# Summing adaLN modulations over partitions with wide ones-matmuls, and fetching their rows earlier

## The chip, the cores and the metric

One Trainium2 chip, one core. The metric is the device time of the program in microseconds (us). Engines are named as in the profile: PE is TensorE (PEld its weight loads), DVE is VectorE, ACT is ScalarE, POOL is GpSimd, SP is SyncE, which here issues DMAs only.

## The reference

A decoder layer with 256 tokens of width 2048, in float32. What matters here is its beginning: a modulation computed from the conditioning vector `c`, applied to the normalised input, and a wide projection of the result.

```python
mod = einsum('bd,de->be', silu(c), w_ada) + b_ada        # w_ada: 2048 x 6144
shift, scale, gate = split(mod[:, None, :], 3, axis=-1)
h = layer_norm(x) * (1.0 + scale) + shift
proj = einsum('bsd,de->bse', h, w_in)                    # w_in: 2048 x 9280
q_lat, kv_lat, mla_gate, pool_in, pool_gate, gate_logits = split(proj, IN_OFFSETS, axis=-1)
...
y = einsum('bsd,de->bse', g_mla * y_mla + g_pool * y_pool, w_out)
x = layer_norm(DEEPNORM_ALPHA * x + (1.0 + gate) * y, ln_g, ln_b)
```

## The kernel before

Each float32 product is made of three fp32r matmuls: an operand is split into a high part (an ACT copy, L108) and a low part (a DVE subtraction, L109), and high x high, high x low and low x high are added up in PSUM (L112 to L114, and with the roles changed L119 to L121).

The 2048 features of `h` are 16 blocks of 128, numbered k = 0 to 15. The product with `w_in` is made in four groups of features, `KGROUPS = ((0, 2), (2, 3), (5, 5), (10, 6))` (first block, number of blocks): here group 0 to group 3. In each group all columns of `w_in` are gone through in blocks of 512; partial sums of earlier groups lie in SBUF and come back into PSUM either by an ACT copy ahead of the matmuls (`seed`, L465) or by a DVE addition behind them (L476). Group 1 ends and group 2 begins at about 154 us of the profile.

Before a group can start, the features in it must have been modulated. `ADA = (((2, 3),), ((5, 3), (8, 2)), ((10, 2), (12, 4)))` says which modulations (first block, number of blocks) are made during groups 0, 1 and 2, for the group that follows; `weave` spreads their jobs over the group's jobs. `ada_jobs(k0, nk)` makes one of them: rows of `w_ada` for these features (shift and scale beside each other) come as raw tiles. DVE multiplies each row by its element of silu(c) and adds it up (L339 for the first rows, L341 for the others) in `acc`, 128 partitions x 2*nk*128 columns. Then `finish`: `fold` sums `acc` over the partitions with one matmul for each 128 columns (weights: 128 x 128 of `acc`; moving operand: one column of ones), so that the result stands as a column in PSUM. A call is two instructions on PE. `modulation` (L348 to L355) adds the bias on DVE and leaves `mod_shift` and `mod_scale`. ACT applies them to the features (L390), and `split` makes the parts `hh` and `hl` that the matmuls read.

The order: `execute` (L155) turns the list of jobs into events (convert a tile, or run a job), and fetches raw tiles on SP in the order in which the events first use them. Five raw tiles are alive at a time (`RAWB`), four converted pairs (`HB`). The rows of `w_ada` and the tiles of `w_in` share these raw tiles and SP's queue. Behind that, a scheduler sets the order of each engine's instructions; on each engine they then run in that order, and one that waits holds all behind it.

Of the kernel before, what the change touches and what calls it, by code (L numbers as in the profile page):

```python
# [9 lines left out]
F32 = mybir.dt.float32  # L10
F32R = mybir.dt.float32r
I32 = mybir.dt.int32
AF = mybir.ActivationFunctionType
ALU = mybir.AluOpType

P = 128
# [15 lines left out]
UNIT = 2048  # L32
HALF = UNIT // 2
RAWB = 5
HB = 4
NCHUNK = 27
NW = 8
# [34 lines left out]
def hybrid_layer(  # L72
# [7 lines left out]
    V, A, T, G = nc.vector, nc.scalar, nc.tensor, nc.gpsimd  # L80

    x, out = x[0], out[0]
# [7 lines left out]
    work = ctx.enter_context(tc.tile_pool(name="work", bufs=2))  # L90
# [3 lines left out]
    def bank():  # L94
        return psum.tile([P, 512], F32, tag="ps", name="ps")
# [5 lines left out]
    def wk(n, name, dt=F32):  # L101
        return work.tile([P, 512], dt, tag="W", name=name, bufs=NW)[:, :n]

    def ck(dt=F32, shape=(P, 4, S), name="ck"):
        return chunk.tile(list(shape), dt, tag="C", name=name)

    def split(src, hi, lo):
        A.activation(hi, src, AF.Copy)  # L108
        V.tensor_tensor(lo, src, hi.bitcast(F32), op=ALU.subtract)  # L109
# [15 lines left out]
    class Raw:  # L125
        def __init__(self, pieces, parts):
            self.pieces, self.left, self.tile = pieces, parts, None

        def fetch(self):
            self.tile = stage.tile([P, UNIT], F32, tag="raw", name="raw", bufs=RAWB)  # L130
            for dst, src in self.pieces(self.tile):
                nc.sync.dma_start(dst, src)

    class Job:
        def __init__(self, fn, raw=None, view=None, pool=None, stacked=False):
            self.fn, self.raw, self.view, self.pool, self.pair = fn, raw, view, pool, None
            self.stacked, self.barrier = stacked, False

        def convert(self):
            src = self.view(self.raw.tile)  # L140
# [3 lines left out]
            else:  # L144
                hi, lo = [stage.tile([P, HALF], F32R, tag=n, name=n, bufs=HB) for n in ("hi", "lo")]
            if self.stacked:
# [8 lines left out]
    def execute(jobs):  # L155
        events = []
        nxt, held = 0, 0
        for i, jb in enumerate(jobs):
            while nxt < len(jobs):
                j = jobs[nxt]  # L160
                if j.barrier and nxt > i:
                    break
                if j.view is None:
                    if j.raw is not None:
                        events.append((1, nxt))
                    nxt += 1
                    continue
                if j.pool is None:
                    if held >= HB:
                        break  # L170
                    held += 1
                events.append((0, nxt))
                nxt += 1
            if jb.raw is None or jb.view is not None:
                events.append((1, i))
            if jb.view is not None and jb.pool is None:
                held -= 1
        order, seen = [], set()
        for kind, i in events:
            r = jobs[i].raw  # L180
            if r is not None and id(r) not in seen:
                seen.add(id(r))
                order.append(r)
        f, live = 0, 0
        for kind, i in events:
            jb = jobs[i]
            while f < len(order) and live < RAWB:
                order[f].fetch()
                f += 1
                live += 1  # L190
            if kind == 0:
                jb.convert()
            else:
                jb.fn(*(jb.pair or ((jb.raw.tile,) if jb.raw is not None and jb.view is None else ())))
                jb.pair = None
            if jb.raw is not None and (kind == 0 or jb.view is None):
                jb.raw.left -= 1
                if jb.raw.left == 0:
                    live -= 1
# [17 lines left out]
    def todo(*fns):  # L217
        return [Job(f) for f in fns]
# [79 lines left out]
    ident = const.tile([P, P], F32, name="ident")  # L298
# [3 lines left out]
    ones_r = const.tile([P, P], F32R, name="ones_r")  # L302
# [40 lines left out]
    def accumulate_raw(acc, raw, per, ui):  # L343
        w = acc.shape[1]
        for i in range(per):
            accumulate(acc, raw[:, i * w:(i + 1) * w], ui * per + i, ui == i == 0)

    def modulation(pa, k0, nk):  # L348
        V.tensor_tensor(
            mod_shift[:, k0:k0 + nk], pa[:, 0:nk], vT[:, VB_ADA + k0:VB_ADA + k0 + nk], op=ALU.add,  # L350
        )
        V.scalar_tensor_tensor(
            mod_scale[:, k0:k0 + nk], pa[:, nk:2 * nk], 1.0,
            vT[:, VB_ADA + KT + k0:VB_ADA + KT + k0 + nk], op0=ALU.add, op1=ALU.add,
        )  # L355


    def fold(pa, acc, first, last):
        n = acc.shape[1] // P
        for j in range(n):  # L360
            T.matmul(
                pa[:, j:j + 1], lhsT=acc[:, j * P:(j + 1) * P], rhs=ones[:, 0:1], start=first and j == 0,
                stop=last, skip_group_check=True,
            )

    def ada_jobs(k0, nk):
        ncol = nk * P
        per = UNIT // (2 * ncol)
        nu = KT // per
        accs = []  # L370

        def unit(raw, ui):
            if ui == 0:
                accs.append((ck(shape=(P, 1024), name="acc") if nk > 2 else wk(512, "acc"))[:, :2 * ncol])
            accumulate_raw(accs[0], raw, per, ui)

        def pieces(t, ui):
            rv = t[:, :per * 2 * ncol].rearrange("p (t s n) -> p t s n", t=per, s=2)
            return [
                (rv[:, :, i, :], w_ada_v[:, ui * per:(ui + 1) * per, i * D + k0 * P:i * D + (k0 + nk) * P])  # L380
                for i in range(2)
            ]

        def finish():
            pa = bank()
            fold(pa, accs[0], True, True)
            modulation(pa, k0, nk)
            for k in range(k0, k0 + nk):
                h = nT[k // 4][:, k % 4, :]
                A.activation(h, h, AF.Identity, scale=mod_scale[:, k:k + 1], bias=mod_shift[:, k:k + 1])  # L390
            k = k0
            while k < k0 + nk:
                e = min(k0 + nk, (k // 4 + 1) * 4)
                if k // 4 == len(hh):
                    hh.append(ck(F32R, name="hh"))
                    hl.append(ck(F32R, name="hl"))
                sl = slice(k % 4, k % 4 + e - k)
                split(nT[k // 4][:, sl, :], hh[k // 4][:, sl, :], hl[k // 4][:, sl, :])
                k = e

        return [
            Job(lambda r, ui=ui: unit(r, ui), Raw(lambda t, ui=ui: pieces(t, ui), 1)) for ui in range(nu)
        ] + todo(finish)

    def rstd_steps(dst, var, eps, ve, t):
        def a(between=lambda: None):
# [119 lines left out]
    def way_in():  # L526
# [47 lines left out]
        def more(n):  # L574
            for _ in range(min(n, len(left))):
                collect(left.pop(0))
# [30 lines left out]
        more(len(left))  # L607
        w_hi, w_lo = zip(*[[stage.tile([P, HALF], F32R, tag=n, name=n, bufs=HB) for n in ("hi", "lo")] for _ in w])
        for q in range(3):
# [259 lines left out]
    scale = float(DQ) ** -0.5  # L869
# [251 lines left out]
    def rows_load():  # L1121
        fin["r"] = stage.tile([P, UNIT], F32, tag="raw", name="rows", bufs=RAWB)[:6, :TC]
        for i in range(6):
            nc.sync.dma_start(fin["r"][i:i + 1], (ln_g, ln_b)[i % 2][0:1, :TC])

    def rows_split():
        rh, fin["rw"] = [
            stage.tile([P, UNIT], F32R, tag="raw", name=n, bufs=RAWB)[:6, :TC] for n in ("rowh", "roww")
        ]
# [109 lines left out]
    for gi, g in enumerate(KGROUPS):  # L1239
        main = chain([  # L1240
            win_tok_jobs(n, cb, *g, gi == 0, gi == 3)
            for n in tok for cb in range(len(tok[n])) if gi or n != "qkv"
        ])
        if gi == 0:
            main[4:4] = todo(lambda: after.close())
        if gi == 1:
            main[1:1] = todo(rope_load)
        if gi < 3:
            J += weave(main, ([j for a in ADA[gi] for j in ada_jobs(*a)], WA[gi], WB[gi]))
        else:  # L1250
            J += weave(main, (todo(rope_tables), 0.0, ROPE), (norm_jobs(), N0, N1), (kpe_jobs(), 0.55, 0.56), (pool_jobs(), P0, P1), (mix_jobs(), M0, M1))
# [37 lines left out]
    for i in behind:  # L1289
        after.enter_context(tc.issue_after(i.ins))  # L1290
    execute(J)


# [34 lines left out]
```

## Time and profile before

| | us |
|---|---|
| median of 3 runs | 800.73 |
| the three runs | 804.12, 800.73, 800.35 |
| the profiled run | 799.99 |
| its span, first to last instruction | 798.1 |
| PE busy in the span | 784.1 |
| DVE busy | 603.9 |
| ACT busy | 501.9 |

How to read the rows: a line such as `L119` is one of the program before. A busy time is from the start of an instruction to its end; matmuls overlap their neighbours, so for a stream of them the distance from start to start is what one costs. In brackets behind a row stands the idle time of its engine just before it, and which instruction or transfer ended that. The granted clock (PEclk) is the share of 2.4 GHz that TensorE was allowed; 0.5 would be 1.2 GHz.

### The profile page before, as it was taken

How to read it: one execution, taken by the hardware profiler on the slowest of the kernel's cores; microseconds unless marked ns; L12 is line 12 of the kernel's file. 1: busy time of each engine (PE TensorE's matmuls, PEld its weight loads, DVE VectorE, ACT ScalarE, POOL GpSimd, SP SyncE). 2: the span in 40 equal slices, each digit the busy share in tenths (PEclk: the TensorE clock that was granted, in tenths of full speed). 3: DMA queues.
4: the chain of work that ended last, by engine and by line, in shares of the span. 5: the costliest groups of instructions: out<-in, count | busy, mean ns of one | idle time of the engine just before them, and what ended most of it. 6: DMA issues, size and time to landing. Idle time of an engine off the chain costs nothing.

```text
span 798.1 us, 11229 instructions
## 1 busy us (share of the span) xinstructions
PE 784.1 (98%) x4146; PEld 674.4 (85%) x4146; DVE 603.9 (76%) x890; ACT 501.9 (63%) x765; POOL 19.0 (2%) x50
## 2 busy tenths in 40 slices
PE   8999999899999999999999999999999999999996
PEld 8788888688887888888888999999998888888885
DVE  7778998776866665467847668887776899769986
ACT  5778656677776889677866676666664344443620
POOL 1000000000000000000100000000000000000050
PEclk9999999999999999999999999999999999999998
DMA  9999998699988766645956545556453979889603
GB/s 305 384 348 340 325 357 292 221 338 314 311 276 302 252 214 203 207 134 165 297 181 207 191 146 199 199 198 199 161 207 108 317 254 348 282 303 383 220 1 105
DMA packets 107642, 195.44 MB, mean 245 GB/s; under 512 B 6922, under 2 KB 32954, under 8 KB 107588
## 3 DMA queue, kind: packets, MB, share of 16 engines
q1 hardware_dynamic: 106724, 192.35, 70.6%
q0 software_dynamic: 640, 2.10, 0.8%
q8 instruction: 32, 0.52, 0.3%
q10 hardware_dynamic: 224, 0.29, 0.1%
q14 instruction: 22, 0.18, 0.1%
HBM read 192.62 MB, written 2.10 MB: 244 GB/s over the span
## 4 chain that ended last, share of the span: by engine, by line
PE 92%; DMA 5%; DVE 2%; issue 0%; SPq 0%; ACT 0%; DVEq 0%; ACTq 0%
PE ps L119 21%; PE ps L121 21%; PE ps L120 21%; PE ps L1184 4%; PE ps L1186 4%; PE ps L1185 4%; PE ps L114 2%; PE ps L112 2%; PE ps L113 2%; DMA raw<-in_w_ada_dram 2%; DMA wa<-in_w_ada_dram 2%; PE ps L281 2%; PE ps L983 1%; PE ps L910 1%; PE ps L911 1%; PE ps L909 1%
## 5 line engine op out<-in xcount | busy, mean ns | idle before, releaser
L109 DVE TENSOR_TENSOR lo<-raw,hi 128x1024 fp32r<-128x1024 f32 (+1 forms) x270 | 308.7, 1150 | 115.3 <-ACT hi L108 106.0
L108 ACT ACTIVATE hi<-raw 128x1024 fp32r<-128x1024 f32 (+1 forms) x272 | 266.4, 987 | 201.9 <-PE ps L120 120.6
L119 PE MATMUL ps<-hi,hh 128*128 128x512 f32 x432 | 169.7, 393 | 3.0 <-ACT ps L465 3.0
L120 PE MATMUL ps<-hi,hl 128*128 128x512 f32 x432 | 168.7, 390 | 0.0
L121 PE MATMUL ps<-lo,hh 128*128 128x512 f32 x432 | 165.6, 391 | 0.3 <-DVE lo L109 0.3
L341 DVE SCALAR_TENSOR_TENSOR acc<-raw,s_c,acc 128x512 f32<-128x512 f32 (+2 forms) x135 | 116.8, 865 | 21.2 <-DMA raw<-in_w_ada_dram 20.1
L119 PEld LDWEIGHTS ps<-hi,hh 128*128 128x128 f32 x432 | 81.6, 189 | 20.0 <-ACT ps L465 3.4
L121 PEld LDWEIGHTS ps<-lo,hh 128*128 128x128 f32 x432 | 81.4, 189 | 17.6 <-DVE lo L109 0.7
L120 PEld LDWEIGHTS ps<-hi,hl 128*128 128x128 f32 x432 | 81.5, 189 | 16.6
L119 PE MATMUL ps<-hi,h 128*128 128x512 f32 x136 | 53.2, 391 | 0.0
L120 PE MATMUL ps<-hi,h 128*128 128x512 f32 x136 | 53.0, 389 | 0.0
L121 PE MATMUL ps<-lo,h 128*128 128x512 f32 x136 | 50.8, 389 | 0.0
L119 PE MATMUL ps<-hi,zh 128*128 128x512 f32 x128 | 50.2, 397 | 0.0
L120 PE MATMUL ps<-hi,zl 128*128 128x512 f32 x128 | 50.1, 392 | 0.0
L121 PE MATMUL ps<-lo,zh 128*128 128x512 f32 x128 | 49.4, 391 | 0.0
L112 PE MATMUL ps<-cn_h,hi 128*128 128x256 f32 x160 | 45.8, 286 | 0.0
L114 PE MATMUL ps<-cn_h,lo 128*128 128x256 f32 x160 | 45.2, 283 | 0.0
L113 PE MATMUL ps<-cn_l,hi 128*128 128x256 f32 x160 | 45.2, 283 | 0.0
L1186 PE MATMUL ps<-hi,ml 128*128 128x512 f32 (+1 forms) x120 | 45.1, 376 | 0.0
L1185 PE MATMUL ps<-lo,mh 128*128 128x512 f32 (+1 forms) x120 | 45.0, 375 | 0.0
L1184 PE MATMUL ps<-hi,mh 128*128 128x512 f32 (+1 forms) x120 | 44.7, 376 | 0.0
L113 PEld LDWEIGHTS ps<-cn_l,hi 128*128 128x128 f32 x160 | 30.6, 191 | 0.1
(286 smaller groups left out, 1262.5 us busy)
## 6 DMA issues: line engine op xcount, KB each, us to landing
raw<-in_w_in_dram SPq DMA_DIRECT2D x44, 1024.0 KB, 8.3
raw<-in_w_ada_dram SPq DMA_DIRECT2D x32, 512.0 KB, 5.1
raw<-in_w_ada_dram SPq DMA_DIRECT2D x16, 1024.0 KB, 5.1
raw<-in_w_mla_o_dram SPq DMA_DIRECT2D x16, 1024.0 KB, 5.1
raw<-in_w_out_dram SPq DMA_DIRECT2D x16, 1024.0 KB, 8.7
raw<-in_w_in_dram SPq DMA_DIRECT2D x18, 768.0 KB, 7.5
raw<-in_w_ada_dram SPq DMA_DIRECT2D x32, 384.0 KB, 5.1
raw<-in_w_in_dram SPq DMA_DIRECT2D x19, 512.0 KB, 3.7
```

Source lines behind the costliest of these rows:

```text
L108: A.activation(hi, src, AF.Copy)
L109: V.tensor_tensor(lo, src, hi.bitcast(F32), op=ALU.subtract)
L112: T.matmul(ps, lhsT=wh, rhs=xh, start=first, stop=False, skip_group_check=True)
L113: T.matmul(ps, lhsT=wh, rhs=xl, start=False, stop=False, skip_group_check=True)
L114: T.matmul(ps, lhsT=wl, rhs=xh, start=False, stop=last, skip_group_check=True)
L119: T.matmul(ps, lhsT=xh, rhs=wh, start=first, stop=False, skip_group_check=True)
L120: T.matmul(ps, lhsT=xl, rhs=wh, start=False, stop=False, skip_group_check=True)
L121: T.matmul(ps, lhsT=xh, rhs=wl, start=False, stop=last, skip_group_check=True)
L341: V.scalar_tensor_tensor(acc, src, s_c[:, t:t + 1], acc, op0=ALU.mult, op1=ALU.add)
L1184: T.matmul(ps, lhsT=xh, rhs=wh[:, k, :], start=first and k == 0, stop=False)
L1185: T.matmul(ps, lhsT=xh, rhs=wl[:, k, :], start=False, stop=False)
L1186: T.matmul(ps, lhsT=xl, rhs=wh[:, k, :], start=False, stop=last and k == 1)
```

## The change

For modulations that start at block 5 or later (`WIDE`), `fold` is replaced by `rows_to_columns`. It takes `acc` in chunks of up to 512 columns. A chunk is split into a high and a low part (ACT copy, DVE subtraction); two fp32r matmuls with a 128 x 128 square of ones as weights and the parts as moving operand leave the sum over partitions in PSUM, the same in every partition. For each 128 columns DVE then multiplies the PSUM square with the identity and adds up along the row, which leaves the diagonal as one column of `pa`, now in SBUF. (5,3) has chunks of 512 and 256 columns, (8,2) and (10,2) one of 512 each, (12,4) two of 512: six chunks, twelve matmuls, 22 squares. The modulation (2,3), and the one that `way_in` makes for blocks 0 and 1, are as before.

Second, `LEAD`: the rows of (5,3) and (8,2) are ordered in SP's queue as though they were used two events earlier.

```diff
+WIDE = 5
+LEAD = {5: 2, 8: 2}
...
-            self.stacked, self.barrier = stacked, False
+            self.stacked, self.barrier, self.lead = stacked, False, 0
...
+        early = sorted(
+            (n - (jobs[i].lead if kind else 0), n)
+            for n, (kind, i) in enumerate(events)
+        )
         order, seen = [], set()
-        for kind, i in events:
-            r = jobs[i].raw
+        for _, n in early:
+            r = jobs[events[n][1]].raw
...
+        def rows_to_columns():
+            pa = work.tile([P, 8], F32, tag="pa", name="pa")
+            for c0 in range(0, 2 * ncol, 512):
+                w = min(512, 2 * ncol - c0)
+                parts = [wk(w, n, F32R) for n in ("acch", "accl")]
+                split(accs[0][:, c0:c0 + w], *parts)
+                ps = bank()
+                for i, a in enumerate(parts):
+                    T.matmul(ps[:, :w], lhsT=ones_r, rhs=a, start=i == 0, stop=i == 1)
+                scratch = wk(w, "scr")
+                for j in range(w // P):
+                    js = slice(j * P, (j + 1) * P)
+                    V.tensor_tensor_reduce(
+                        out=scratch[:, js], in0=ps[:, js], in1=ident, scale=1.0, scalar=0.0, op0=ALU.mult,
+                        op1=ALU.add, accum_out=pa[:, c0 // P + j:c0 // P + j + 1],
+                    )
+            return pa
+
         def finish():
-            pa = bank()
-            fold(pa, accs[0], True, True)
+            if k0 >= WIDE:
+                pa = rows_to_columns()
+            else:
+                pa = bank()
+                fold(pa, accs[0], True, True)
             modulation(pa, k0, nk)
...
-        return [
-            Job(lambda r, ui=ui: unit(r, ui), Raw(lambda t, ui=ui: pieces(t, ui), 1)) for ui in range(nu)
-        ] + todo(finish)
+        jobs = [Job(lambda r, ui=ui: unit(r, ui), Raw(lambda t, ui=ui: pieces(t, ui), 1)) for ui in range(nu)]
+        for jb in jobs:
+            jb.lead = LEAD.get(k0, 0)
+        return jobs + todo(finish)
```

The scheduler also orders the engines anew. ACT where group 2 begins, before: the last tile conversions (`hi`), the modulation of blocks 8 and 9 applied (`nT`), the first seed copy of group 2 (`ps_1615`, of the column block `qkv`), the high part `hh` of the new features, and the second seed copy.

```order
L108 ACTIVATE hi<-raw 128x1024 x2
L390 ACTIVATE nT<-nT,mod_shift,mod_scale 128x256 x2
L465 COPY ps_1615<-qkv 128x512
L108 ACTIVATE hh<-nT 128x512
L108 ACTIVATE hi<-raw 128x512
L465 COPY ps_1617<-qkv 128x512
L478 COPY gm<-ps_1559 128x512
```

The same place now (line numbers are two to thirty higher; L495 is the seed, L419 the application, L508 the copy of a finished block):

```order
L110 ACTIVATE hi<-raw 128x1024 x2
L495 COPY ps_1639<-qkv 128x512
L495 COPY ps_1641<-qkv 128x512
L508 COPY gm<-ps_1583 128x512
L495 COPY ps_1686<-qkv 128x512
L110 ACTIVATE hi<-raw 128x512
L110 ACTIVATE hi<-raw 128x1024
L508 COPY gm<-ps_1585 128x512
L495 COPY ps_1688<-qkv 128x512
L419 ACTIVATE nT<-nT,mod_shift,mod_scale 128x256 x2
```

The seed copies of the first two column blocks of group 2 have moved ahead of the modulation.

DVE at the same place, before: low parts of tiles (`lo`), the first multiply with rows of (10,2) (L339), a low part, the second rows (L341), and the modulation of (8,2).

```order
L109 TENSOR_TENSOR lo<-raw,hi 128x512
L109 TENSOR_TENSOR lo<-raw,hi 128x1024
L109 TENSOR_TENSOR lo<-raw,hi 128x512
L339 TENSOR_SCALAR acc<-raw,s_c 128x512
L109 TENSOR_TENSOR lo<-raw,hi 128x1024
L341 SCALAR_TENSOR_TENSOR acc<-raw,s_c,acc 128x512
L349 TENSOR_TENSOR mod_shift<-ps,vT 128x2
L352 SCALAR_TENSOR_TENSOR mod_scale<-ps,vT 128x2
```

Now, first where the accumulated rows of (8,2) are split (`accl`) and the first of the four squares (L404; the row behind it is the read of the accumulator):

```order
L111 TENSOR_TENSOR accl<-acc,acch 128x512
L506 TENSOR_TENSOR gm<-ps_1565,gm 128x512
L506 TENSOR_TENSOR gm<-ps_1566,gm 128x512
L111 TENSOR_TENSOR lo<-raw,hi 128x1024 x2
L404 ISA scr,pa<-ps,ident 128x128
L404 ISA pa 128x1
```

And from the last of the four squares to the modulation of (8,2):

```order
L404 ISA scr,pa<-ps,ident 128x128
L404 ISA pa 128x1
L346 TENSOR_SCALAR acc<-raw,s_c 128x512
L111 TENSOR_TENSOR lo<-raw,hi 128x512
L356 TENSOR_TENSOR mod_shift<-pa,vT 128x2
L359 SCALAR_TENSOR_TENSOR mod_scale<-pa,vT 128x2
```

The first multiply with rows of (10,2) still stands ahead of the modulation, but two low parts that stood behind it stand ahead of it. On SP each tile of rows of (5,3) and (8,2) stands one tile of `w_in` earlier than before, and from the end of group 1 on the sequence is the same.

## Rows read from the trace of the kernel before

**Rows 1.** The page: busy time of PE, and the chain that ended last.

```profile
PE 784.1 (98%) x4146; PEld 674.4 (85%) x4146; DVE 603.9 (76%) x890; ACT 501.9 (63%) x765; POOL 19.0 (2%) x50
...
PE 92%; DMA 5%; DVE 2%; issue 0%; SPq 0%; ACT 0%; DVEq 0%; ACTq 0%
```

**Rows 2.** PE's timeline at the end of group 1: start us, us, operation.

```profile
153.76 0.39 PE L121 MATMUL ps<-lo,hh 128*128 128x512 f32 x1
157.13 0.50 PE L119 MATMUL ps<-hi,hh 128*128 128x512 f32 x1 [2.99 <-ACT ps L465]
...
157.94 0.58 PE L119 MATMUL ps<-hi,hh 128*128 128x512 f32 x1
...
160.45 1.05 PE L119 MATMUL ps<-hi,hh 128*128 128x512 f32 x2
...
161.82 0.39 PE L119 MATMUL ps<-hi,hh 128*128 128x512 f32 x1
...
162.95 0.39 PE L121 MATMUL ps<-lo,hh 128*128 128x512 f32 x1
```

**Rows 3.** Stretches: length, busy PE, PEld, DVE, ACT, POOL; PEclk, DMA share, GB/s.

```profile
110.00:150.00 40.00, 40.00 (x188) 33.49 (x187) 33.79 (x47) 28.15 (x44) 0.19 (x1) 1.00 0.90 301
...
157.20:161.90 4.70, 4.70 (x14) 3.70 (x15) 4.26 (x6) 4.39 (x8) 0.00 (x0) 0.64 0.64 215
```

**Rows 4.** Timeline of all engines, 145 to 158 us (SPq: a DMA issue).

```profile
145.58 0.92 SPq L132 DMA_DIRECT2D raw<-in_w_ada_dram  x2
...
148.55 0.95 PE L361 MATMUL ps<-ones,acc 128*128 128x1 f32 x8
...
153.05 0.49 DVE L339 TENSOR_SCALAR acc<-raw,s_c 128x512 f32<-128x512 f32 x1 [5.16 <-DMA raw<-in_w_ada_dram]
...
155.26 0.15 DVE L349 TENSOR_TENSOR mod_shift<-ps,vT 128x2 f32<-128x2 f32 x1
...
155.51 1.09 ACT L390 ACTIVATE nT<-nT,mod_shift,mod_scale 128x256 f32<-128x256 f32 x2 [5.70 <-DVE mod_scale L352]
156.51 0.58 ACT L465 COPY ps<-qkv 128x512 f32<-128x512 f32 x1
...
157.83 0.92 SPq L132 DMA_DIRECT2D raw<-in_w_ada_dram  x2
```

**Rows 5.** The chain of waits, one piece: start us, us, what.

```profile
146.00 6.96 DMA raw<-in_w_ada_dram
```

**Rows 6.** PE's timeline at the fold of (5,3), and matmuls with 256 columns.

```profile
114.98 1.17 PE L361 MATMUL ps<-ones,acc 128*128 128x1 f32 x10
116.01 0.48 PE L119 MATMUL ps<-hi,h 128*128 128x512 f32 x1
116.33 0.40 PE L120 MATMUL ps<-hi,h 128*128 128x512 f32 x1
...
466.99 0.28 PE L113 MATMUL ps<-cn_l,hi 128*128 128x256 f32 x1
...
467.11 0.28 PE L114 MATMUL ps<-cn_h,lo 128*128 128x256 f32 x1
```

**Rows 7.** DVE's timeline: a low part of 512, and reductions with their reads.

```profile
121.94 0.68 DVE L109 TENSOR_TENSOR lo<-raw,hi 128x512 fp32r<-128x512 f32 x1
122.54 0.75 DVE L341 SCALAR_TENSOR_TENSOR acc<-raw,s_c,acc 128x512 f32<-128x512 f32 x1
...
467.17 0.29 DVE L955 CUSTOM_DVE_ANT_0 sb<-ps,sb 128x128 f32<-128x128 f32 x1
467.39 0.08 DVE L955 DVE_READ_ACCUMULATOR2_ANT st<- 128x1 f32 x1
467.39 0.42 DVE L955 CUSTOM_DVE_ANT_0 sb<-ps,mask 128x256 f32<-128x256 f32 x1
```

**Rows 8.** Timelines of ACT and DVE late in group 2.

```profile
245.75 1.06 ACT L108 ACTIVATE hi<-raw 128x1024 fp32r<-128x1024 f32 x1 [4.27 <-DMA raw<-in_w_in_dram]
...
249.31 1.28 DVE L341 SCALAR_TENSOR_TENSOR acc<-raw,s_c,acc 128x1024 f32<-128x1024 f32 x1 [1.24 <-DMA raw<-in_w_ada_dram]
```

## The prediction, made before the changed kernel was run

> **What bounds the kernel now.** I read the page first: TensorE is busy for 98% of the span and holds 92% of the chain that ended last [rows 1]. Time can therefore only be won where PE does work that could be spared, where it stands still, or where its clock is low. PE's timeline has one place in the stage of `w_in` where the last two come together [rows 2]. The last matmul of group 1 (features 2 to 4) starts at 153.76 us and, at the usual 0.227 us from start to start (161.82 to 162.95 is five of them), is through at 153.99. The next starts only at 157.13: 3.14 us lost. From there the granted clock is 0.64 on average [rows 3], which is a mixture of 2.4 GHz and its lower level, 1.2 GHz: between 157.94 and 160.45 the matmuls start 0.42 us apart. The 13 matmuls from 157.13 to 161.82 take 4.69 us where 13 x 0.227 = 2.95 would do: 1.74 lost. Together the place costs **4.88 us**.
>
> Why PE stands still is read backwards from it [rows 4]. Its matmul waits for the ACT copy that seeds the PSUM bank (L465, 156.51). Ahead of that copy in ACT's order stand the two activations that apply the modulation of features 8 and 9 (L390, 155.51), and these wait for DVE's `mod_shift` and `mod_scale` at 155.26. The sums over partitions that these two need were on PE at 148.55, six microseconds before. What holds DVE is its own order: ahead of the modulation stands the first multiply with rows of the *next* features, 10 and 11 (L339), and it sat 5.16 us until its rows landed, at 152.96 in the chain [rows 5]. Their transfer was issued at 145.58. So three orders (DVE, ACT, SP) make the stall, and not a lack of speed in any engine.
>
> **Part 1: sums on PE.** What goes are 22 calls of `fold`, 44 records on PE, in five places of 10, 2, 8, 8 and 16. Start to start, ten take 114.98 to 116.01 = 1.03 us [rows 6], so 0.103 us each and 4.5 in all. The matmul behind each place is late too: 116.01 to 116.33 is 0.32 where 0.227 is usual, 0.09 x 5 = 0.45. Removed: **4.95**. Added are 12 matmuls of the same fp32r kind as the rest, ten with 512 columns and two with 256: 10 x 0.227 + 2 x 0.12 = **2.5** (with 256 columns the trace has 466.99 to 467.11 = 0.12, [rows 6]). PE runs without gaps there, so all of it lies on the path: **-2.45**, between -2.0 (if nothing but the folds' own 4.5 comes back) and -2.6.
>
> Here a rule of the Trainium skill speaks against the change. The trace shows 0.10 us for each fold record [rows 6]. "TensorE: Matmul & The Clock Gate", section "Back-to-back issue gap", gives a matmul of 1 to 64 columns some 60 cycles, about 25 ns, against 518 cycles for 512 columns; by it the estimate would be 44 x 0.025 = 1.1 us removed against 2.4 added, and PE would lose 1.3. The row decides against it: each fold loads another 128x128 of weights, and the same page's section "LDWEIGHTS (loading the stationary operand)" gives such a load 107 ns, with which the row agrees. The wide form loads one set of ones for 512 columns instead.
>
> **Part 2: work added on DVE and ACT.** Six chunks are split into two parts: ACT copies of about 0.58 us each, like the seed copy of 128x512 in [rows 4], 3.5 us in all; ACT is not near its bound, and the copies stand where it otherwise waits. DVE subtracts: 0.68 long [rows 7], 0.60 from start to start, five of these and a half one are 3.4. Then 22 reductions of a 128x128 square out of PSUM, each with a read of the accumulator. The trace has such a pair [rows 7]: 0.29 long, with the next instruction 0.22 after its start and the 0.08 read beside that. So 22 x 0.22 = 4.8 at the least and 22 x 0.37 = 8.1 at the most, if nothing overlaps; I take 0.22, since the row is of the same kind and size. DVE gets **8.2 us** (up to 12). In group 1, where it counts, (5,3) and (8,2) bring three splits and ten squares: 1.55 + 2.2 = 3.8 us, at most 5.4. DVE is busy 33.79 of the 40 us from 110 to 150 [rows 3], so 6.2 are free there (2 of them in the block at L339, which began at 147.9). I price it at nothing on the path, with cover of 6.2 - 3.8 = 2.4 us; if the cover is gone, PE waits for `lo` tiles by what is over.
>
> The squares also break a rule of the skill. The row shows 0.22 us from one to the next [rows 7]. "VectorE: DVE Perf Modes", section "The TRN2 errata", says that a fixed latency is paid by each instruction and advises tiles of 512 elements and more; its `120 + FD` cycles for a PSUM source give, as an estimate, 0.26 us for a square and 5.7 for 22 of them. By it DVE would get one microsecond more than I sum, which its free time still covers.
>
> **Part 3: rows fetched earlier, and the orders.** On SP each tile of rows for features 5 to 9 now stands one `w_in` tile earlier; the sequence behind is the same. The earlier rows push single `w_in` tiles back by a slot: the first of group 1 by about a microsecond, with two to three to spare before PE wants it. The first tile of (10,2) waits in SP for a buffer that the accumulation of (8,2) frees; walked through with the durations of before, that accumulation ends some 2 us earlier, so the tile is issued at about 143.5 instead of 145.58 and lands at about 150.5 instead of 152.96 (6.96 us in [rows 5]).
>
> The new order matters more than the slot. On ACT both seed copies of the first block of group 2, and those of the second, stand before the modulation is applied. On PE, 34 matmuls of group 2 that use features 5 to 7 alone come before the first that needs features 8 and 9: 34 x 0.227 = 7.7 us of work. Group 1 ends on PE at about 153 (the folds of this stage are cheaper by about one). The second ones-matmul of (8,2) stands four matmuls before that end, so its PSUM is ready at about 152.2, the four squares at 153.1, the multiply with rows of (10,2) (landed by then) and a `lo` tile at 154.2, then the modulation, the two activations (1.09 long in [rows 4]) and the copy of `hh`: ready at about 157, or 157.6 with ACT's queue ahead. PE wants it at 153 + 7.7 = 160.7. The block still stands before the modulation on DVE, but there are about 3 us in hand, and both `lo` tiles that PE needs meanwhile now stand ahead of the block. So **the whole 4.88 goes**, the slow clock with the stall that came before it. Next late would be the `lo` tile of the second block (ready about 156.3, wanted 157.8). For small waits of this kind I give back 0.45.
>
> **Sum.** -4.88 - 2.45 + 0.45 = -6.88 on the profiled run of 799.99 us (span 798.1): 793.1. The median of the three runs is 0.74 above the profiled one; against it, **793.9 us**.
>
> **Rivals.**
> *The stall stays.* If the rows of (10,2) land after about 155, DVE's block again holds the modulation past 160. For it: the block is still in front, and the wait was 5.16 once. Against it: the 34 matmuls of cover. Then only Part 1 is left: 800.73 - 2.45 = 798.3.
> *The gain is given back further on.* Late in group 2 ACT waits 4.27 us for a `w_in` tile at 245.75 and DVE 1.24 for rows at 249.31 [rows 8]. If that supply does not move forward with PE, PE meets it 6 to 7 us early and waits there. Against it: SP issues when buffers come free, which PE's pace sets, and the next rows go out earlier as well, at about 152 where SP stood idle until 157.83 [rows 4]. Time: one microsecond under before at best, 799.7.
> *The folds were cheap.* If the squares of weights were hidden, as the page's gap of 25 ns would have it, PE loses by the wide matmuls. From rows: the lowest price for the removed part is nothing but the late matmuls, 0.45, against 2.5: -4.88 + 2.05 + 0.45 = -2.4, so 798.3; 797.7 if part of it counts.
> *DVE becomes the bound (slower).* Place: 110 to 153 us. If reductions and reads do not overlap, DVE's extra work there is 5.4; if the free time falls where no work is ready, all of it delays `lo` tiles, PE waits 5.4 in that stage, and the stall with its slow clock stays and a second slow stretch of 1.74 comes: 800.73 - 2.45 + 5.4 + 1.74 = 805.4. It decides from where DVE's extra work no longer fits the 4.2 us that are free in bits before the block at L339 (6.2 less 2). Against it: the 0.22 in [rows 7].
>
> **How the numbers follow.** What a measurement of this kernel can tell from no change is 0.5%, 4.0 us: faster is below 796.7, slower above 804.7. My forecast has 0.66 (its own range 792.4 to 796.5: PE's term to -2.6, no give-back, or half of the stall left). The stall that stays has 0.12, the gain given back 0.10, cheap folds 0.03: these three lie within 0.5%. DVE as the bound has 0.09. So faster 0.66, same 0.25, slower 0.09. The range must reach the first two rivals' near side: 792.4 to 799.0 leaves out DVE's case, most of the given-back case and little at the bottom.
>
> **What would show it.** Right: on PE no wait for ACT at the start of group 2, granted clock 1.00 through 150 to 165, twelve ones-matmuls at 0.23 and 0.12 with no late one behind, PE's busy time about 4 us lower (2.45, and 1.74 of slow clock). The squares at 0.22 on DVE; the modulation of (8,2) behind the first multiply of (10,2) but before 156. Wrong: a wait of PE for `hh` near 160, for `lo` between 110 and 157, or of over 2 us in 234 to 282; an accumulation of (8,2) that ends no earlier than before; a granted clock under 1.00 in any of these.

## The result, and the profile after

The changed kernel takes 794.06 us in the median of four runs (792.82 to 795.23); the kernel before took 802.42 on the same chip (median of four, 800.35 to 804.79). The ratio is 0.9897, 95% interval [0.9867, 0.9927]: about 8 us faster. A second set of runs of the same kernel (below) gave 794.49 and 0.9898 [0.9865, 0.9931].

The page of the changed kernel (span 793.0 us, profiled run 794.77) against [rows 1]: PE is busy for 99% of the span, and what DMA and DVE had of the chain that ended last (5% and 2%) is down to 1% each.

```profile
PE 781.9 (99%) x4114; PEld 673.8 (85%) x4114; DVE 612.5 (77%) x940; ACT 503.2 (63%) x771; POOL 19.0 (2%) x50
...
PE 97%; DVE 1%; DMA 1%; SPq 0%; ACT 0%; issue 0%; DVEq 0%; ACTq 0%
```

The stretches that answer to [rows 3] (length, busy PE, PEld, DVE, ACT, POOL; PEclk, DMA share, GB/s):

```profile
110.00:150.00 40.00, 40.00 (x179) 33.08 (x178) 38.50 (x65) 29.15 (x47) 0.00 (x0) 1.00 0.93 309
150.00:157.20 7.20, 7.20 (x34) 5.92 (x32) 5.72 (x18) 5.21 (x8) 0.00 (x0) 1.00 0.90 310
157.20:161.90 4.70, 4.70 (x22) 3.92 (x21) 4.27 (x5) 4.17 (x7) 0.00 (x0) 1.00 1.05 360
```

PE works through the change of groups, and the clock stays at 1.00. PE's timeline there, against [rows 2]: group 1 ends with 155.38, group 2 begins 0.23 us later, and the first matmuls with features 8 and 9 (163.32, two in one row) come without a wait.

```profile
154.69 0.39 PE L400 MATMUL ps<-accl,ones_r 128*128 128x512 f32 x1
154.92 0.39 PE L121 MATMUL ps<-hi,hh 128*128 128x512 f32 x1
...
155.38 0.39 PE L123 MATMUL ps<-lo,hh 128*128 128x512 f32 x1
155.61 0.39 PE L121 MATMUL ps<-hi,hh 128*128 128x512 f32 x1
...
163.32 0.62 PE L121 MATMUL ps<-hi,hh 128*128 128x512 f32 x2
```

One thing has to be taken out before the two profiles are compared. They begin differently, at a place that the change does not touch: the first matmul of the product with `w_in` in the queue of jobs starts at 33.17 us in the profile before and at 35.85 in this one. Behind the product nothing differs (from the start of the first transpose of `pi` to that of the last matmul 450.0 to 450.1 us in every profile of this case). So I measure the **stretch** between these two points, in PE's timeline: 341.76 - 33.17 = 308.59 us before, 336.63 - 35.85 = 300.78 after, **7.81 us less**. Going through the timelines of both from one start to the next, and adding up what is over 0.227 us for each matmul, gives where they come from:

| in the stretch, group 1 on | before, us | after, us |
|---|---|---|
| folds, 44 records | 4.49 | - |
| late matmuls behind them | 0.46 | none over 0.02 |
| wait at the start of group 2 | 3.14 | 0 |
| slow clock behind it | 1.74 | 0 |
| wait for a low part at 251.8, with the late matmul behind it | 0.56 | 0 |
| ones-matmuls, 10 x 0.227 + 2 x 0.113 | - | 2.49 |

The difference of the columns is 10.39 - 2.49 = 7.90.

### The profile page after: what moved, and what is told of

The parts are those of the page before. It is cut to its first block, busy times and chain, and to the rows that moved or that the text cites. A ratio compares the mean times of both kernels' runs of the same rounds, so it can differ in the third digit from the quotient of the medians.

```text
span 793.0 us, 11210 instructions
## 1 busy us (share of the span) xinstructions
PE 781.9 (99%) x4114; PEld 673.8 (85%) x4114; DVE 612.5 (77%) x940; ACT 503.2 (63%) x771; POOL 19.0 (2%) x50
## 4 chain that ended last, share of the span: by engine, by line
PE 97%; DVE 1%; DMA 1%; SPq 0%; ACT 0%; issue 0%; DVEq 0%; ACTq 0%
PE ps L121 22%; PE ps L122 22%; PE ps L123 22%; PE ps L1216 4%; PE ps L1214 4%; PE ps L1215 4%; PE ps L116 2%; PE ps L114 2%; PE ps L115 2%; PE ps L288 2%; PE ps L1013 1%; PE ps L940 1%; PE ps L941 1%; PE ps L939 1%; DMA x<-in_x_dram 1%; PE ps L975 1%
## 5 line engine op out<-in xcount | busy, mean ns | idle before, releaser
L123 PE MATMUL ps<-lo,hh 128*128 128x512 f32 x432 | 163.9, 389 | 0.0
```

The source lines that it names most:

```text
L123: T.matmul(ps, lhsT=xh, rhs=wl, start=False, stop=last, skip_group_check=True)
```

## Experiments

Each ran beside the kernel before on the same chip; the stretch is that of one profile of each. Before: 308.59.

| kernel | median, us | ratio to before, 95% | stretch, us | against before |
|---|---|---|---|---|
| the change | 794.06 | 0.9897 [0.9867, 0.9927] | 300.78 | -7.81 |
| e1, wide sums alone | 798.49 | 0.9953 [0.9932, 0.9975] | 305.21 | -3.38 |
| e2, earlier rows alone | 797.81 | 0.9954 [0.9936, 0.9973] | 303.12 | -5.47 |
| e3, wide sums in group 2 alone | 799.17 | 0.9963 [0.9948, 0.9977] | 307.27 | -1.32 |
| e4, next rows later | 798.45 | 0.9957 [0.9935, 0.9980] | 305.33 | -3.26 |
| e5, squares twice | 796.77 | 0.9937 [0.9916, 0.9957] | 304.90 | -3.69 |
| e5, squares four times | 803.59 | 1.0019 [0.9998, 1.0039] | 311.32 | +2.73 |
| e6, wide sums for (2,3) too | 801.91 | 0.9997 [0.9983, 1.0011] | 309.31 | +0.72 |
| e7, longer warm-up | 795.35 | 0.9911 [0.9880, 0.9942] | 302.38 | -6.21 |
| e8, wide sums, jobs earlier | 795.15 | 0.9913 [0.9882, 0.9943] | 302.66 | -5.93 |
| e9, the change again | 794.49 | 0.9898 [0.9865, 0.9931] | 300.72 | -7.87 |
| e10, two longer warm-ups | 794.26 | 0.9904 [0.9870, 0.9937] | 300.72 | -7.87 |

Ratio and stretch do not always agree: by its ratio e2 gains 2.2 to 5.1 us (stretch 5.47) and e3 1.8 to 4.2 (stretch 1.32). A stretch is read from a single profile, and two profiles of one program exist for the change alone (300.78 and 300.72), so that how much the others vary is not shown.

### e1: the wide sums without the earlier rows

```diff
-LEAD = {5: 2, 8: 2}
+LEAD = {}
```

> The wide sums alone, rows fetched as in the kernel before (LEAD empty). My theory: the stall of 4.88 us at the start of group 2 is a matter of order; here too both pairs of seed copies stand ahead of the applied modulation on ACT, and 34 matmuls of group 2 come before one that needs features 8 and 9. So the stall goes without the earlier rows, and PE's term of -2.45 stands: 7.3 to 7.9 us under the kernel before, no wait of PE for ACT, granted clock 1.00 at the start of group 2, within 1 us of the full change. Rival (the earlier rows are what removes the stall): the rows of (10,2) land late as before, PE waits about 3 us again, and only about 2.5 us are gained.

My theory fell: the stretch is 4.43 us longer than with both parts. The seed copies stand ahead of the applied modulation on ACT as I described it, PE goes into group 2 at once, and stops further on, at the first matmul with the new features. PE's timeline:

```profile
160.02 0.40 PE L400 MATMUL ps<-accl,ones_r 128*128 128x512 f32 x1
...
164.29 0.62 PE L123 MATMUL ps<-lo,hh 128*128 128x512 f32 x2
166.48 1.19 PE L121 MATMUL ps<-hi,hh 128*128 128x512 f32 x4 [1.57 <-ACT hh L110]
168.01 0.59 PE L122 MATMUL ps<-hi,hl 128*128 128x512 f32 x1 [0.34 <-DVE hl L111]
168.39 0.63 PE L123 MATMUL ps<-lo,hh 128*128 128x512 f32 x1
```

The first row is the second ones-matmul of (8,2). Only 18 matmuls stand between it and the first with the new features; in the changed kernel (154.69 and 163.32) there are 37. So PE's order is not that of the change here, and the squares could not have come before this matmul was through, at 160.4.

From 160 to 172 us the matmuls lose 4.5 us in all, since the clock falls again (from 168.39 they start 0.43 apart). DVE's timeline says why the features are later still:

```profile
159.56 1.23 DVE L111 TENSOR_TENSOR lo<-raw,hi 128x1024 fp32r<-128x1024 f32 x1 [3.20 <-ACT hi L110]
162.03 1.23 DVE L111 TENSOR_TENSOR lo<-raw,hi 128x1024 fp32r<-128x1024 f32 x1 [1.24 <-ACT hi L110]
163.17 0.28 DVE L404 CUSTOM_DVE_ANT_0 scr<-ps,ident 128x128 f32<-128x128 f32 x1
```

Here the squares of (8,2) stand behind two low parts of a tile of `w_in`, and in the chain of waits this tile is the late one: it could be issued only when the accumulation of (8,2) had freed a raw buffer (that ended at 151.1, where in the changed kernel it ended at 147.4), and took 7.32 us.

```profile
151.12 7.32 DMA raw<-in_w_in_dram
```

So the modulation again stands on DVE behind something that waits for a transfer: another instruction and another transfer, the same form of stall. The wide sums alone move the stall further into group 2; they do not remove it. What share the late ones-matmul has in it, and what the tile, this run does not separate.

### e2: the earlier rows without the wide sums

```diff
-WIDE = 5
+WIDE = 99
```

> The earlier rows alone, fold on every modulation (WIDE out of reach). My theory: the rows of (8,2) are summed earlier, and the modulation stands ahead of the first multiply with rows of (10,2) on DVE and ahead of a seed copy of group 1 on ACT; the stall and its slow clock go (-4.9, and perhaps -0.5 of the small wait at 251.8), the folds stay at 0.10 us a record with a late matmul behind each: 4.9 to 5.5 us under the kernel before, some 2.5 slower than the full change. Rival (cheap folds): the same time as the full change or less, since the folds cost nothing and the wide matmuls 2.5. Rival (the wide sums remove the stall, by their place in the order): no gain.

As expected in the profile: 5.47 us less, no wait of PE in the whole stretch, all 44 fold records there (4.57 us with the same 0.09 to 0.10 behind each place). With the rows earlier the scheduler puts the modulation ahead of the first multiply with rows of (10,2), and both far ahead of the first seed copy of group 2. Timeline of DVE and ACT:

```profile
148.33 0.15 DVE L359 SCALAR_TENSOR_TENSOR mod_scale<-ps,vT 128x2 f32<-128x2 f32 x1
...
149.00 0.48 DVE L346 TENSOR_SCALAR acc<-raw,s_c 128x512 f32<-128x512 f32 x1
...
152.91 0.58 ACT L495 COPY ps<-qkv 128x512 f32<-128x512 f32 x1
```

The ratio (0.9954, 3.7 us) is less than the stretch of the profiled run, which at 796.44 was among the quicker ones of the ten. Cheap folds would have made this kernel as fast as the change or faster: the changed kernel's stretch is 2.34 us shorter.

### e3: the wide sums only where they cannot touch the stall

```diff
-WIDE = 5
-LEAD = {5: 2, 8: 2}
+WIDE = 10
+LEAD = {}
```

> Wide sums only for the modulations of group 2, (10,2) and (12,4), rows fetched as before. The order up to the start of group 2 is that of the kernel before, so the stall of 3.1 us and the slow clock behind it stay. What is measured is PE's term alone: 24 fold records at 0.10 and two late matmuls go (2.7), six matmuls of 0.227 come (1.36): 1.3 us under the kernel before, up to 1.9 if the wait at 251.8 goes too. Rival (cheap folds, 25 ns a record): 0.6 us slower than before.

1.32 us less in the stretch, where 1.3 was expected, with the stall in place:

```profile
155.48 0.39 PE L123 MATMUL ps<-lo,hh 128*128 128x512 f32 x1
158.38 0.80 PE L121 MATMUL ps<-hi,hh 128*128 128x512 f32 x1 [2.51 <-ACT ps L495]
158.97 0.63 PE L122 MATMUL ps<-hi,hl 128*128 128x512 f32 x1
```

The agreement is partly luck: the stall with its slow clock is 4.13 us here where it was 4.88, and small waits at 252 to 257 add 0.7 in exchange. What holds without them is the timeline itself: fold records are 0.10 apart in every profile, ones-matmuls 0.23.

### e4: one number, no other sums and no earlier rows

```diff
-WA = (0.05, 0.0, 0.0, 0.0)
+WA = (0.05, 0.0, 0.02, 0.0)
```

> The kernel before with one number changed: the rows of (10,2) and (12,4) are spread over group 2 from 2% on and not from its start. Folds as before, no row earlier. It puts the modulation of (8,2) ahead of the first multiply with rows of (10,2) on DVE, and changes nothing in how the sums are made. My theory (the stall is DVE's order: an instruction that waits for a transfer ahead of the modulation): the stall goes, 4 to 5.4 us under the kernel before, PE's fold records unchanged. Rival (the stall comes from the sums being slow or late on PE, or from the transfers): it stays, and the time is that of before.

The stall is gone: the largest distance between two starts on PE from 151 to 160 us is that of a single matmul, and neither the sums nor the transfers are faster. So it was DVE's order. But the rows that begin later also end up closer together, and later in group 2 PE waits for low parts that stand on DVE behind multiplies that wait for rows. PE, and then DVE:

```profile
235.41 0.50 PE L121 MATMUL ps<-lo,hh 128*128 128x512 f32 x1 [0.74 <-DVE lo L109]
...
249.76 0.50 PE L121 MATMUL ps<-lo,hh 128*128 128x512 f32 x1 [0.48 <-DVE lo L109]
```

```profile
239.71 1.28 DVE L341 SCALAR_TENSOR_TENSOR acc<-raw,s_c,acc 128x1024 f32<-128x1024 f32 x1 [2.25 <-DMA raw<-in_w_ada_dram]
...
247.29 1.29 DVE L341 SCALAR_TENSOR_TENSOR acc<-raw,s_c,acc 128x1024 f32<-128x1024 f32 x1 [2.23 <-DMA raw<-in_w_ada_dram]
```

Waits between 234 and 251 cost 2.15 us where they cost 0.56 before: 4.88 - 1.59 = 3.29 of gain, and 3.26 measured. That is much like my second rival (the gain is given back further on), seen in a neighbour of the change.

### e5: more squares, to find DVE's edge

```diff
-                for j in range(w // P):
+                for j in [j for j in range(w // P) for _ in range(2 if k0 < 10 else 1)]:
```

> The changed kernel, with each diagonal square of (5,3) and (8,2) taken twice (the second writes the same result again): ten more squares on DVE in group 1, 10 x 0.21 = 2.1 us. My theory (DVE has cover in group 1, some 2.4 us by the sum in the prediction): the stretch from the first matmul of the product with w_in to the first transposes of pi stays within 0.5 us of the changed kernel's 300.8. Rival (DVE is at its bound there): 2 us longer.

The same line with 4 in place of 2:

> The same with each of these squares taken four times: 30 more, 6.3 us of DVE in group 1. It is to find the edge that the slower rival of the prediction speaks of. My theory: the cover of some 2.4 us is passed, PE waits for low parts or for the new features by what is over, 4 us, and with a slow clock behind a wait of over 1.5 us as much as 6: 302 to 307 us for the stretch that takes 300.8 in the changed kernel. Rival (DVE's waits are far larger than I counted): no change.

2.1 us more on DVE made the stretch 4.1 us longer, and 6.3 made it 10.5 longer (311.3, where I had allowed 302 to 307). Both theories fell. With twice as many squares PE's waits in the table of waits are (engine, line, waited for: total, times, longest):

```profile
PE ps L123 <- DVE lo L111: 1.6, 1, 1.6
...
PE ps L121 <- ACT hh L110: 0.8, 1, 0.8
PE ps L121 <- DVE gm L506: 0.7, 1, 0.7
```

and with four times as many:

```profile
PE ps L121 <- ACT hh L110: 6.4, 2, 4.7
...
PE ps L400 <- DVE accl L111: 1.0, 1, 1.0
```

These are not pure prices of DVE time, for the scheduler orders these kernels differently (repeated squares stand among other work). With twice as many squares the longest wait, 1.6 us at 172.25, is for a low part that DVE began at 170.98, as soon as ACT had its high part ready; just before, DVE itself had stood idle for 2.99 us for rows. DVE's time was not what was short there, and with the late matmul behind it this place is 1.8 of the 4.1 us. The wait for `hh` ends with two things at once, at 161.1 to 161.2: DVE's `mod_scale`, which stands behind the squares, and a high part that stands ahead on ACT. So the kernels with more squares are slower; how much of that is DVE's time, and how much cover the changed kernel has left, is not shown.

### e6: the wide sums for (2,3) as well

```diff
-WIDE = 5
+WIDE = 2
```

> The changed kernel with the wide sums for (2,3) too: twelve fold records at 0.103 and a late matmul of 0.09 go (1.33), four matmuls come (2 x 0.227 + 2 x 0.115 = 0.68), six squares on DVE in group 0. By PE's term 0.65 us less in the stretch that takes 300.8 in the changed kernel. Rival: group 1 waits for features 2 to 4, which come later by the squares, and a wait of one to three microseconds appears at its start.

The rival, and more of it than its one to three microseconds: 8.5 us longer than the change. PE waits at the start of group 1, and the clock falls behind it:

```profile
85.55 0.80 PE L121 MATMUL ps<-hi,h 128*128 128x512 f32 x1 [5.12 <-ACT gm L504]
```

The ACT copy that it waits for stands behind the applied modulation of (2,3), and that behind DVE's `mod_scale` at 82.43:

```profile
82.43 0.15 DVE L359 SCALAR_TENSOR_TENSOR mod_scale<-pa,vT 128x3 f32<-128x3 f32 x1
```

A second chunk of 256 columns has to be split and squared there, between the low parts of tiles. For the 0.65 us of PE that were expected that is a bad bargain; leaving (2,3) with `fold` is part of what makes the change work.

### e8: the wide sums, with the jobs earlier and not the fetches

```diff
-LEAD = {5: 2, 8: 2}
+LEAD = {}
...
-WB = (0.85, 0.85, 0.85, 0.8)
+WB = (0.85, 0.75, 0.85, 0.8)
```

> Wide sums with no rows fetched ahead of their turn (LEAD empty), but the jobs of the modulations (5,3) and (8,2) woven in so that they end at 75% of group 1 and not at 85%. With the wide sums alone the stall came back further on, 1.6 us for the new features and a slow clock: the accumulation of (8,2) ended late, the next tile of w_in came late behind it, and the squares stood on DVE behind two low parts of that tile. My theory: what removes the stall is that the accumulation of (8,2) ends early, by whatever means; here the squares stand ahead of those low parts again, and the stretch from the first matmul with w_in to the transposes of pi is within 1 us of the changed kernel's 300.8. Rival (only the order of the fetches on SP does it, or DVE is too full without it): 303 us and more, with a wait of PE for the new features.

No wait at the start of group 2 and none for the new features. The accumulation of (8,2) ended at 144.8 here, so an early end of it is enough, and SP's order is one way to it. In the middle of group 1, however, 1.9 us are lost, most of it at

```profile
137.45 0.50 PE L121 MATMUL ps<-hi,h 128*128 128x512 f32 x1 [1.01 <-ACT hi L110]
```

PE waits there for a high part of a tile. On ACT the modulation of (5,3), three activations, and its `hh` now stand ahead of that high part, and ACT works without a pause from 130.65 on:

```profile
132.65 1.59 ACT L419 ACTIVATE nT<-nT,mod_shift,mod_scale 128x256 f32<-128x256 f32 x3
...
136.34 1.58 ACT L110 ACTIVATE hi<-raw 128x1024 fp32r<-128x1024 f32 x2
```

So the stretch is 302.66, 1.9 us over the changed kernel's, where I had allowed one.

### e7, e9, e10: the start of the program

```diff
-SPIN = (54, 26, 8, 10, 8, 2, 2)
+SPIN = (54, 38, 8, 10, 8, 2, 2)
```

> The changed kernel with twelve more transposes (26 to 38) in the warm-up of PE ahead of the first use of x; nothing else. The profiles differ at the start: where the warm-up ended at 12.2 us, PE then waited 2 us for x and its granted clock was 0.50 from 15 to 25 us, and the product with w_in began 2.7 us later than where it ended at 13.7. My theory: this makes the spread between runs of both kernels, and twelve transposes (1.4 us) keep PE at work until x is there: the slow stretch goes, runs lie closer together, and the median is 0.5 to 1.5 us under that of the changed kernel. Rival: the late warm-up is delayed by 1.4 us less the 0.6 it waited, and the median is up to 0.8 us slower.

The changed kernel once more:

> The changed kernel once more, for a second profile with another start and for more times beside the kernel before. My theory: the stretch with w_in is 300.8 us whatever the start was, with no wait of PE at the start of group 2; the time lies 7 to 9 us under that of the kernel before. Rival (the margins of one to three microseconds that I counted are used up by a start that falls otherwise): some of the runs show a wait for the new features or for low parts, and the stretch is one to five microseconds longer.

And both warm-ups longer:

```diff
-SPIN = (54, 26, 8, 10, 8, 2, 2)
+SPIN = (54, 38, 8, 10, 14, 2, 2)
```

> The changed kernel with twelve more transposes ahead of the first use of x (26 to 38) and six more ahead of the last rows of the first modulation (8 to 14). With the first twelve alone one profile still had a slow stretch from 26 to 33 us, behind waits of 0.55 and 0.35 us for rows and their sum. My theory: filling both keeps the clock at 1.00 to the end of the start in all runs; the product with w_in begins at 33 to 34 us, and the median is 1 to 2 us under the changed kernel's. Rival (the extra transposes only delay what follows, and the clock falls where it falls): no gain, up to 1 us slower.

e9 repeats the stretch: 300.72 us, no wait, from a start that lay 3.6 us earlier. The longer warm-ups don't pay: medians of 795.35 and 794.26 against 794.06 and 794.49 for the change. Nor do the runs of e7 lie closer together (793.6 to 797.15).

In e7 the stretch is 1.6 us longer than in the change, though nothing in it was edited. The scheduler put the instructions behind the warm-up in a somewhat different order, and late in group 2 PE waits for low parts that stand on DVE behind multiplies that wait for rows. DVE, and then PE:

```profile
247.41 1.28 DVE L348 SCALAR_TENSOR_TENSOR acc<-raw,s_c,acc 128x1024 f32<-128x1024 f32 x1 [1.45 <-DMA raw<-in_w_ada_dram]
```

```profile
249.88 0.50 PE L123 MATMUL ps<-lo,hh 128*128 128x512 f32 x1 [0.39 <-DVE lo L111]
```

Whether the order or the late start (36.60) brings this about is not shown. It means that between two differently ordered kernels some 1.6 us of stretch can come without any cause in the edited part. In e10 the single times lie closer together (793.47 to 795.63; the change again 791.12 to 795.9), its clock was 1.00 from 5 to 25 us and fell behind the next wait, to 0.66 from 25 to 30. That profiles of one program differ at the start is shown (below); that a longer warm-up helps is not.

## Why the prediction was right, and where it was not

**The time** was 793.9 foretold and 794.06 measured, inside the range; that the two are so close is luck, for two things that I had too small cancel in it. The gain was put at 6.88 us; in the stretch it is 7.81 and by the ratio 8.3 (5.9 to 10.7). And the profile and median that I started from lie low: over the 31 runs beside e1 to e4 the kernel before has a median of 802.34, not 800.73. Probably that is because the start in its profile was an early one (33.17 us; the profiles with this warm-up show 32.28 to 36.46).

**The stall, -4.88: right**, with its cause. It is gone in the change, and e4 removes it with one number, which begins the rows of (10,2) later, so that their first multiply stands behind the modulation on DVE.

**PE's term, -2.45: right.** 4.49 + 0.46 - 2.49 = 2.46 in the timelines; the change is 2.34 us ahead of e2, which like it has no wait of PE, but has the folds. The ones-matmul with 512 columns is 0.23 from start to start, with 256 it is 0.11 (126.75 to 126.86):

```profile
126.75 0.28 PE L400 MATMUL ps<-acch,ones_r 128*128 128x256 f32 x1
126.86 0.39 PE L123 MATMUL ps<-lo,h 128*128 128x512 f32 x1
```

The row was the better guide here. By an estimate from the 25 ns that "TensorE: Matmul & The Clock Gate" of the Trainium skill, section "Back-to-back issue gap", gives for a narrow matmul (44 x 0.025 = 1.1 us removed, 2.49 added), the change over e2 would have been a loss of 1.4 us; the trace shows a gain of 2.34. That section says itself that its gap leaves out the loading of weights, so that it speaks against the change less than the prediction has it.

**The squares, 0.22 each: right**, 0.21 with the read beside the next one. DVE's timeline at (8,2), with the three instructions that decide when the features are modulated:

```profile
155.12 0.29 DVE L404 CUSTOM_DVE_ANT_0 scr<-ps,ident 128x128 f32<-128x128 f32 x1 [0.55 <-PE ps L400]
155.33 0.08 DVE L404 DVE_READ_ACCUMULATOR2_ANT pa<- 128x1 f32 x1
155.33 0.28 DVE L404 CUSTOM_DVE_ANT_0 scr<-ps,ident 128x128 f32<-128x128 f32 x1
...
155.97 0.48 DVE L346 TENSOR_SCALAR acc<-raw,s_c 128x512 f32<-128x512 f32 x1
...
156.97 0.15 DVE L356 TENSOR_TENSOR mod_shift<-pa,vT 128x2 f32<-128x2 f32 x1
```

The multiply with rows of (10,2) still stands ahead of the modulation, and no longer waits. On the clock of the profile before (2.68 us less) the modulation is at 154.3, and I had written "a `lo` tile at 154.2, then the modulation". The copy `hh` ends at 161.4, on that clock 158.7, 1.1 later than the 157.6 that I had, because ACT waited for a tile of `w_in` that stands ahead of it:

```profile
156.74 1.06 ACT L110 ACTIVATE hi<-raw 128x1024 fp32r<-128x1024 f32 x1 [1.40 <-DMA raw<-in_w_in_dram]
...
158.84 1.09 ACT L419 ACTIVATE nT<-nT,mod_shift,mod_scale 128x256 f32<-128x256 f32 x2
...
160.78 0.62 ACT L110 ACTIVATE hh<-nT 128x512 fp32r<-128x512 f32 x1
```

PE takes it at 163.32, that is at 160.64 (foretold: 160.7). The margin was 1.9 us, not 3.

**The rows of (10,2) came earlier, but by less, and not for the reason given.** The accumulation of (8,2) ended at 147.4 (144.7 on the clock of before, where it was 145.6): 0.9 us earlier, not 2. The first tile of (10,2) went out at 146.76 (144.1 on that clock; 143.5 foretold), freed by a low part that DVE made from 146.06 to 146.74. That was early enough: DVE's multiply did not wait for it. SP's issues of the first and the second tile:

```profile
146.76 1.70 SPq L134 DMA_DIRECT2D raw<-in_w_ada_dram  x2
...
154.60 0.92 SPq L134 DMA_DIRECT2D raw<-in_w_ada_dram  x2
```

**DVE's cover: wrong.** I priced DVE's new work at nothing, with 6.2 - 3.8 = 2.4 us to spare. The price was right: PE waited nowhere. The cover was not, and the step that failed is reading it from a sum of idle time. Of the 6.2 us idle from 110 to 150, 2.1 lay in the block at L339, that is, in the stall itself, and went with it. The stretch that PE was working on from 110 to 150 in the changed kernel is 107.32 to 147.32 in the kernel before:

```profile
107.32:147.32 40.00, 40.00 (x184) 33.34 (x183) 35.90 (x51) 25.84 (x42) 0.00 (x0) 1.00 0.90 303
```

There DVE had 4.1 us free, about the 4.2 that the prediction itself counts in its slower rival; less 3.8 that leaves 0.3, not 2.4. With 38.50 busy the changed kernel has 1.5 left in this window, in which only six of the ten squares fall. So by this count the slower rival had its edge nearer than Part 2 put it. Where it lies is not shown: e5 with ten squares more lost 4.1 us, not all of them to DVE's time, and with 30 more the gain was gone (ratio 1.0019 [0.9998, 1.0039]).

**"The new order matters more than the slot": not borne out.** The order on ACT is not enough: in e1, without the earlier rows, the seed copies stand ahead of the modulation, and 4.5 us are lost. But the slot made part of the order, for without it the ones-matmul of (8,2) stands later on PE and its squares later on DVE, so that the two can't be weighed against each other. The earlier rows decide when the accumulation of (8,2) ends, and with it when its squares can be made and when the next tile of `w_in` can be fetched; e8 reaches the same by earlier jobs. By the stretch the wide sums are worth 3.4 us alone and 2.3 on top of the earlier rows; the earlier rows 5.5 alone and 4.4 on top. By the ratios they are worth about the same, 3.8 and 3.7 alone.

**PE's busy time**, foretold about 4 us lower, is 2.2 lower in the first profile (784.1 to 781.9) and 5.3 lower in that of e9 (778.8): the start, which differs between them, is in it.

**The 0.45 given back: wrong in sign.** No small wait came, and the one of 0.56 at 251.8 went, probably because SP could fetch on where it had stood idle (the second tile of (10,2) is issued at 154.60, on the clock of before at 151.9; I had 152, and before it was 157.83 [rows 4]). With 4.88 + 2.45 + 0.56 the sum would have been 7.89.

## What to carry to other kernels

Before an engine is called too slow, look at what stands in front of the late instruction in its own queue: here a multiply that waited for a transfer of the next stage held the last step of this one, and one number that moves it took the stall away, though a third of the gain was lost again further on. Moving work to an engine that is not the bound needs cover at the place where its results are due, not in the sum, least of all in a sum that holds the idle time of the very stall that is to go; the same wide sums that pay for (5,3) to (12,4) cost 8.5 us when (2,3) has them too. And when two profiles are compared, first find a point in each from which nothing but the change differs: here the start of one program varied by 3.6 us, almost half of the gain. And where a scheduler orders the engines anew, a small edit may move more than it names (e1, e5, e7).

## What the runs showed of the hardware that I had not expected

The start differs between executions of one program: the first matmul of the stretch came at 35.85 us in one profile of the changed kernel and at 32.28 in the other, 3.6 us apart (32.28 to 36.46 over all kernels with this warm-up). PE warms up with 54 and then 26 transposes. In the profile after they were through at 12.2 us, PE waited 1.98 us for `x`, and from 15 to 25 us its granted clock was 0.50, the lower level; in e9, the same program, they were through later, the wait was 0.93 us, and the clock stayed at 1.00. The stretch from 15 to 25 us and PE's first use of `x`, of the change and then of e9:

```profile
15.00:25.00 10.00, 10.00 (x50) 10.00 (x49) 6.26 (x9) 5.86 (x8) 0.00 (x0) 0.50 1.08 370
```

```profile
14.14 1.33 PE L474 MATMUL ps<-ident,x 128*128 128x128 f32 x8 [1.98 <-ACT x L464]
```

```profile
15.00:25.00 10.00, 9.48 (x84) 8.82 (x82) 7.68 (x11) 7.95 (x11) 0.00 (x0) 1.00 1.08 370
```

```profile
14.32 1.09 PE L474 MATMUL ps<-ident,x 128*128 128x128 f32 x8 [0.93 <-ACT x L464]
```

Nor does the length of a wait alone tell whether the clock falls. In e1 it fell behind a wait of 1.57 us (0.68 from 166.5 to 171.4), in e5 with twice the squares it stayed at 1.00 behind one of 1.57:

```profile
166.50:171.40 4.90, 4.56 (x13) 3.27 (x14) 4.41 (x7) 1.27 (x2) 0.00 (x0) 0.68 0.89 279
```

```profile
172.20:178.00 5.80, 5.75 (x25) 4.75 (x26) 5.51 (x7) 2.27 (x4) 0.00 (x0) 1.00 0.80 257
```

What else decides it, these runs don't show.
